# Queries and keys of two heads as block products through DRAM, with earlier copies out of PSUM and a later small load

## The chip, the cores and the metric

The kernel runs on one core of one Trainium2 chip. The metric is the device time in microseconds, the median of several runs; lower is better. Names in the rows: PE is the matrix engine (TensorE), PEld its weight load, DVE the vector engine, ACT the scalar engine, POOL and SP the two engines that issue the transfers (DMA).

## The reference

One step of a two-layer encoder on 576 tokens (64 of a running stream, 512 of a new one), width 2048, 16 heads of 128. Layer A is chunk-band attention with normed queries and keys, layer B attention over compressed keys and values; each layer adds its gated, projected result to its input.

```python
def a_project(h, w_in, g_q, g_k):
    q, k, v, g = jnp.split(h @ w_in, 4, axis=-1)
    hd = (b, s, A_HEADS, A_HEAD_DIM)
    return rmsnorm(q.reshape(hd), g_q), rmsnorm(k.reshape(hd), g_k), v.reshape(hd), g
...
    q, k, v, g = a_project(rmsnorm(x, ln), w_in, g_q, g_k)
    ...   # scores with a relative bias, softmax over the band, times v
    y = x + (jax.nn.silu(g) * o) @ w_out
    return y, k, v          # keys and values are outputs too
```

## The kernel before

Everything lies transposed, features in the 128 partitions and the 576 tokens along the free axis as two halves of 288. A float32 product is made of three products of rounded parts (high times high, low times high, high times low), so a **plain projection** of one 128-column tile is 16 k-tiles x 3 products x 2 halves = 96 matmuls of 128x288. Two such column tiles can be made together as a **block pair** (`block_pairs`): seven products of sums of blocks instead of eight, 7 x 8 x 3 = 168 matmuls instead of 192. Its inputs are sums of blocks of the activations, formed once beside earlier products (`block_operands`, tiles aiT, boT), and of the weights.

The stages of layer A: values and gates of heads 0 and 1 together (`values_and_gates`, banks av0, av1, ag0, ag1; ending at 60 us), the column sums of the layer norm (lnast) and their root chain, value and gate of head 2 as plain projections (ap34, ap50), then 13 block pairs (ai35 to ai47, to 393 us), each a value tile and a gate tile that are stored to DRAM (vd, sgd). After that `head_a` runs for each of 16 heads: queries and keys as plain projections (`proj`, a0p0, a0p1, ...), each with its norm (`qk_chain`: squares, sums over the partitions on PE as a00st, a01st, root, scaling, split into high and low parts qh, ql, kh, kl), the value loaded back from DRAM and transposed (`v_chain`), and the attention, whose pieces are laid between the projections of later heads. Then the output projection, layer B in the same style, and its output projection `out_b`: bo0 to bo3 plain, with the residual added (L1322), the other 12 tiles as block pairs bo4, bo6, ... .

PE's order is written out by hand: a small planner (`Order`) runs these routines as streams. A stream yields a bank class it needs ("mm": 2 banks of two halves, "st": 1, "x": 2), a time or a condition, and gets on when that is free by the planner's own clock; `od_.give` returns a bank after an assumed delay. The other engines' instructions are put in order by the scheduler of the language, and each engine and each queue works strictly in its order. Tiles come from pools with a fixed number of buffers for each tag, and a load into a tile waits until the buffer's last reader is done. In the head stage the tag raw (queries, keys and values) has 3 buffers.

Of the kernel before, what the change touches and what calls it, by code (L numbers as in the profile page):

```python
# [15 lines left out]
F32 = mybir.dt.float32  # L16
# [102 lines left out]
def encoder(tc, xT, wa_in, wa_out, wb_in, wuq, wuk, wuqr, wuv, wb_out, kcT, vc, ckvcT, krcT, gains, rtab,  # L119
# [26 lines left out]
    vd = dram.tile([D, N], F32, name="vd")  # L146
    sgd = dram.tile([D, N], F32, name="sgd")
    qrd = dram.tile([D, N], F32, name="qrd")
    qd = dram.tile([D, N], F32, name="qd")
# [493 lines left out]
    h, xs = [], []  # L643
    state = {"ln": 0.0, "scored": -1, "in": False}

# [40 lines left out]
    def out_of(m, src, y):  # L686
        (value_of if m < MG else gate_a)(m, src, y)

# [9 lines left out]
    def values_and_gates():  # L698
# [6 lines left out]
        for kt in range(KT):  # L705
            hi, lo = ws.get(3)
            for w in range(4):
                s = slice(w * P, (w + 1) * P)
                mm3(outs[w], (hi[:, s], lo[:, s]), [[x[:, c * 288:(c + 1) * 288] for x in h[kt]] for c in range(2)],
                    kt == 0, kt == KT - 1)  # L710
            yield None
            if kt + 4 < KT:
                load_x(kt + 4)
            square_sum(acc, xs[kt], tpx, N, kt == 0, f"lna{kt}")
        g1 = y_tile(MG + 1)
        ACT.copy(two(g1), pg1[:, :, :288])
# [5 lines left out]
        od_.spawn(1, stats_a(acc))  # L722
        for j in range(2):
            od_.spawn(1, later(MV + j, pv[j][:, :, :288], y_tile(MV + j), "mm"))
        od_.spawn(1, later(MG, two(g0), g0, None))
# [10 lines left out]
        for _ in form:  # L736
# [3 lines left out]
        pools.append(g_w1)  # L740
        yield from block_pairs(wa_in, X, [(MV + j, MG + j) for j in range(3, H)],
                               lambda name: wp1.tile([P, WH], F32, tag="o", bufs=10, name=name), None, y_tile,
# [22 lines left out]
    o2 = [None] * H  # L765
    ws = Weights(wload, [p for hd in range(H) for w in range(2) for p in parts_of(wa_in, [w * H + hd], "wa")], 2)

    def head_a(hd):
# [4 lines left out]
        def qk_chain(which, ps):  # L773
            col = gak if which else gaq
            raw = raw_of(ps, tpa, N, f"{n_}raw{which}")
            if which:
                kc = ap_.tile([P, NC], F32, tag="kc", bufs=2, name=n_ + "kc")
                nc.sync.dma_start(kc, kcT[hd * P:(hd + 1) * P, :])
            yield lambda: state["ln"]
            st = yield from halves(raw, tpa, N, f"{n_}{which}")  # L780
            t0 = max(od_.now, state["ln"] - 2.0)
            z = rnorm(st, P, N, base=EX, coef=P * EPS / D)
            scaled(raw, col, z)
            yield lambda: state["scored"] >= hd - 1
            if which == 0:
                hi = ap_.tile([P, N], F32R, tag="qh", bufs=1, name=n_ + "qh")
                lo = ap_.tile([P, N], F32R, tag="ql", bufs=1, name=n_ + "ql")
                split(raw, hi, lo)
            else:
                nc.gpsimd.dma_start(kT[hd * P:(hd + 1) * P, :], raw)  # L790
                hi = ap_.tile([P, NK], F32R, tag="kh", bufs=1, name=n_ + "kh")
                lo = ap_.tile([P, NK], F32R, tag="kl", bufs=1, name=n_ + "kl")
                split(raw, hi[:, NC:], lo[:, NC:])
                split(kc, hi[:, :NC], lo[:, :NC])
            yield max(t0 + L_RN, od_.now + L_SP)
            got[which] = hi, lo

        def v_chain():
            vt = tpa("raw", F32, n_ + "vt")
            nc.gpsimd.dma_start(vt, vd[hd * P:(hd + 1) * P, :])  # L800
# [14 lines left out]
            split(tps, vh, vl)  # L815
            od_.give("x", L_T)
            got["v"] = vh, vl, vs

# [4 lines left out]
        def bias():  # L823

            T = ap_.tile([P, 256], F32, tag="T", bufs=2, name=n_ + "T")
            nc.sync.dma_start(T, rtab[hd * P:(hd + 1) * P, :])
# [31 lines left out]
        for which in range(2):  # L858
            yield "mm"
            ps = ps_of("mm", f"{n_}p{which}")  # L860
            yield from proj(ps, ws, h, N)
            od_.spawn(1, qk_chain(which, ps))
# [171 lines left out]
    def rotary_key(ps):  # L1034
# [6 lines left out]
        split(raw, KR[0][:, NC:], KR[1][:, NC:])  # L1041
        cc = lp.tile([P, NC], F32, tag="cc", bufs=1, name="krc")
        nc.gpsimd.dma_start(cc, krcT)
# [257 lines left out]
    def pair_b(j):  # L1301

        t = []
        for kt in (j, j + 8):
            t.append(bo.tile([P, N], F32, tag="o", bufs=16, name=f"bf{kt}"))
            nc.gpsimd.dma_start(t[-1], od[kt * P:(kt + 1) * P, :])
        return t

    oB = Ahead((pair_b(j) for j in range(8)), 5)
    X, form_b, last_b = block_operands(lambda j: oB.get(), o2, bo, "bo")  # L1310

    def out_b():
        for m in range(4):
# [7 lines left out]
            y = out_tile_b(m)  # L1321
            V.tensor_tensor(out=two(y), in0=ps[:, :, :288], in1=two(xr), op=ALU.add)  # L1322
            od_.give("mm", L_M)
            done_b(m, y)
        last_b()
# [11 lines left out]
L_VT, L_G, L_CQ, L_M, L_V, L_LN, L_HA, L_LB = 5.0, 5.8, 10.0, 1.5, 5.0, 5.0, 8.0, 4.0  # L1337
ATT = "t0 s2 t1 s3 o-1 t2 t3"
DIRECT, GA, WRAW, WHL, SGB, DEEP, VA = 2, 2, 3, 5, 2, 2, 2
LAT = (0, 1, 2, 3, 8, 4, 5, 6, 7, 9, 10)  # L1340
# [86 lines left out]
```

## Time and profile before

| | us |
|---|---|
| median of 3 runs (2007.34 to 2012.24) | 2010.94 |
| the profiled execution | 2007.77 |
| its span, first to last instruction | 2005.9 |
| PE busy | 1956.2 (98%) |
| DVE busy | 1491.2 (74%) |
| ACT busy | 1180.6 (59%) |

The profile shows one execution. A row of a timeline has the start, the duration, the engine, the line, the operation with its output and inputs, and in brackets how long the engine sat idle before it and what ended that. Chains are read backwards: what ended last, and what released it. The granted clock is the share of full speed that PE had in a stretch.

### The profile page before, as it was taken

Reading aid. Unit: us, or ns where it says so; the run is one execution under the profiler, and the core shown is the slowest. Engines: PE = TensorE matmul, PEld = TensorE weight load, DVE = VectorE, ACT = ScalarE, POOL = GpSimd, SP = SyncE. Lnnn points to the kernel's source line nnn. Section 1 sums busy time; section 2 is a strip of 40 time slices with the busy share of each in tenths; the row PEclk is TensorE's granted clock in tenths of the full one; section 3 lists DMA queues with packets and bytes.
Section 4 is the critical chain, followed back from the end, with each engine's and each line's share of the span. In section 5 each row is a group of like instructions: output and inputs, shape, how many; then the busy total and the mean of one; then the engine's idle time right before and its main releaser. Section 6 shows DMA issues by size and latency. Waiting matters only on the chain.

```text
span 2005.9 us, 37809 instructions
## 1 busy us (share of the span) xinstructions
PE 1956.2 (98%) x14380; PEld 1932.3 (96%) x14380; DVE 1491.2 (74%) x2935; ACT 1180.6 (59%) x2214; POOL 136.9 (7%) x258
## 2 busy tenths in 40 slices
PE   8699999999999999999999899999999999999998
PEld 8699999999999999998999899999999999999998
DVE  8778888757777777779887648887776766776875
ACT  7655555556656565665544538986765666564332
POOL 1100000020000000000000200000000000002000
PEclk9899999999999999999999899999999999999999
DMA  7534444353222323222543525553222322256542
GB/s 232 190 117 135 141 133 134 120 198 92 91 91 88 98 81 99 84 92 66 190 148 108 182 80 147 161 165 117 78 84 88 91 86 83 83 153 222 168 143 64
DMA packets 125446, 247.00 MB, mean 123 GB/s; under 512 B 15808, under 2 KB 30160, under 8 KB 125264
## 3 DMA queue, kind: packets, MB, share of 16 engines
q1 hardware_dynamic: 104288, 171.46, 28.8%
q0 software_dynamic: 20976, 73.13, 10.5%
q8 instruction: 113, 1.85, 0.4%
q14 instruction: 69, 0.57, 0.1%
HBM read 198.07 MB, written 43.79 MB: 121 GB/s over the span
## 4 chain that ended last, share of the span: by engine, by line
PE 86%; issue 8%; DVE 2%; DMA 2%; ACT 1%; POOL 0%; SPq 0%; POOLq 0%; DVEq 0%; ACTq 0%
PE g L166 8%; PE lat L166 7%; PE u L166 4%; PE ao L166 2%; PE ap L166 1%; PE av L166 1%; PE a15p L166 1%; PE a14p L166 1%; PE a13p L166 1%; PE a12p L166 1%; PE a10p L166 1%; PE a9p L166 1%; PE a8p L166 1%; PE a7p L166 1%; PE a6p L166 1%
## 5 line engine op out<-in xcount | busy, mean ns | idle before, releaser
L206 DVE TENSOR_TENSOR wa_2l<-wa_2r,wa_2h 128x512 fp32r<-128x512 f32 x35 | 24.2, 691 | 19.7 <-ACT wa_2h L205 19.6
L205 ACT CAST wa_2h<-wa_2r 128x512 fp32r<-128x512 f32 x35 | 21.7, 620 | 21.4 <-PE a3p L166 1.9
L205 ACT CAST wa_0h<-wa_0r 128x512 fp32r<-128x512 f32 x35 | 21.5, 614 | 21.5 <-PE a0p L166 3.2
L206 DVE TENSOR_TENSOR wa_0l<-wa_0r,wa_0h 128x512 fp32r<-128x512 f32 x35 | 23.9, 684 | 11.7 <-ACT wa_0h L205 11.6
L206 DVE TENSOR_TENSOR wa_3l<-wa_3r,wa_3h 128x512 fp32r<-128x512 f32 x35 | 24.1, 687 | 11.1 <-ACT wa_3h L205 11.1
L206 DVE TENSOR_TENSOR wb_1l<-wb_1r,wb_1h 128x512 fp32r<-128x512 f32 x25 | 17.2, 688 | 15.0 <-ACT wb_1h L205 15.0
L166 PE MATMUL u<-cqh,wq_0h 128*128 128x288 f32 x128 | 27.7, 298 | 0.5 <-ACT q6raw L500 0.3
L205 ACT CAST wa_3h<-wa_3r 128x512 fp32r<-128x512 f32 x35 | 21.3, 609 | 10.4 <-PE a0p L166 4.4
L166 PE MATMUL u<-cqh,wq_0l 128*128 128x288 f32 x128 | 27.4, 296 | 0.0
L166 PE MATMUL u<-cql,wq_0h 128*128 128x288 f32 x128 | 27.3, 295 | 0.0
L206 DVE TENSOR_TENSOR wb_3l<-wb_3r,wb_3h 128x512 fp32r<-128x512 f32 x25 | 17.2, 687 | 13.2 <-ACT wb_3h L205 13.2
L166 PE MATMUL lat<-bh,wb_0h 128*128 128x288 f32 x88 | 19.9, 309 | 6.3 <-ACT bh L210 6.3
L205 ACT CAST wb_3h<-wb_3r 128x512 fp32r<-128x512 f32 x25 | 15.4, 616 | 17.8 <-PE lat L166 8.1
L205 ACT CAST wb_1h<-wb_1r 128x512 fp32r<-128x512 f32 x25 | 15.5, 618 | 17.5 <-PE lat L166 8.8
L206 DVE TENSOR_TENSOR wa_1l<-wa_1r,wa_1h 128x512 fp32r<-128x512 f32 x35 | 24.1, 689 | 2.0 <-ACT wa_1h L205 1.5
L166 PE MATMUL g<-bh,wb_1h 128*128 128x288 f32 x112 | 24.3, 298 | 0.0
L166 PE MATMUL g<-bh,wb_0h 128*128 128x288 f32 x112 | 24.3, 298 | 0.0
L166 PE MATMUL g<-bh,wb_2h 128*128 128x288 f32 x112 | 24.2, 298 | 0.0
L166 PE MATMUL g<-bh,wb_3h 128*128 128x288 f32 x112 | 24.2, 298 | 0.0
L166 PE MATMUL g<-bh,wb_0l 128*128 128x288 f32 x112 | 24.0, 296 | 0.0
L166 PE MATMUL g<-bh,wb_1l 128*128 128x288 f32 x112 | 24.0, 296 | 0.0
L166 PE MATMUL g<-bl,wb_1h 128*128 128x288 f32 x112 | 24.0, 296 | 0.0
(8217 smaller groups left out, 8616.4 us busy)
## 6 DMA issues: line engine op xcount, KB each, us to landing
wa_0r<-wa_in SPq DMA_DIRECT2D x34, 256.0 KB, 3.0
wa_1r<-wa_in SPq DMA_DIRECT2D x34, 256.0 KB, 3.1
wa_2r<-wa_in SPq DMA_DIRECT2D x34, 256.0 KB, 2.9
wa_3r<-wa_in SPq DMA_DIRECT2D x34, 256.0 KB, 3.0
wb_0r<-wb_in SPq DMA_DIRECT2D x25, 256.0 KB, 3.2
wb_1r<-wb_in SPq DMA_DIRECT2D x25, 256.0 KB, 3.2
wb_2r<-wb_in SPq DMA_DIRECT2D x25, 256.0 KB, 3.1
wb_3r<-wb_in SPq DMA_DIRECT2D x25, 256.0 KB, 2.9
```

Of the source, the lines that this page charges most:

```text
L166: nc.tensor.matmul(out, lhs, rhs, start=start, stop=stop, **kw)
L205: ACT.copy(hi, src)
L206: V.tensor_tensor(out=lo, in0=src, in1=hi.bitcast(F32), op=ALU.subtract)
```

## The change

- Heads 0 and 1 (`EARLY`) get their queries and keys from two more block pairs, (0, 16) and (1, 17), after the 13; `out_of` stores these raw to a new DRAM array qkd. Their four plain projections go, and `qk_chain` loads the raw tile from qkd (new tag rawd, 2 buffers) on POOL's queue.
- New conditions for the planner: at most 2 chains and 3 raws at a time, values in the order of the heads; the value tile has a buffer of its own (vt, 1), the bias table T 1 instead of 2.
- The first value's bank av0 is copied out by ACT with high priority, before the statistics; its scaling then reads the copy.
- The rotary key's cached part krc is loaded into a tile of the tag sw.
- In `out_b` the bank of bo0 to bo3 is copied out by ACT, and the residual is added afterwards from the copy; the tiles bf are all allocated at the start.

```diff
@@ -145,6 +145,7 @@
     od = dram.tile([D, N], F32, name="od")
     vd = dram.tile([D, N], F32, name="vd")
     sgd = dram.tile([D, N], F32, name="sgd")
+    qkd = dram.tile([2 * D, N], F32, name="qkd")
     qrd = dram.tile([D, N], F32, name="qrd")
     qd = dram.tile([D, N], F32, name="qd")
 
@@ -641,7 +642,7 @@
 
     ws = Weights(wload4, [(kt,) for kt in range(KT)], 2)
     h, xs = [], []
-    state = {"ln": 0.0, "scored": -1, "in": False}
+    state = {"ln": 0.0, "scored": -1, "in": False, "chains": 0, "raws": 0, "v": -1}
 
     def load_x(kt):
         x = tpx("x", F32, f"x{kt}")
@@ -684,7 +685,10 @@
         nc.gpsimd.dma_start(sgd[hd * P:(hd + 1) * P, :], y)
 
     def out_of(m, src, y):
-        (value_of if m < MG else gate_a)(m, src, y)
+        if m < MV:
+            nc.gpsimd.dma_start(qkd[m * P:(m + 1) * P, :], y)
+        else:
+            (value_of if m < MG else gate_a)(m, src, y)
 
     def y_tile(m):
         return tpy("y", F32, f"y{m}")
@@ -712,6 +716,10 @@
             if kt + 4 < KT:
                 load_x(kt + 4)
             square_sum(acc, xs[kt], tpx, N, kt == 0, f"lna{kt}")
+        v0 = y_tile(MV)
+        with tc.high_priority():
+            ACT.copy(two(v0), pv[0][:, :, :288])
+        od_.give("mm", L_M)
         g1 = y_tile(MG + 1)
         ACT.copy(two(g1), pg1[:, :, :288])
         od_.give("st", L_M)
@@ -720,8 +728,8 @@
             ACT.copy(g0[:, c * 288:(c + 1) * 288], pg0[c][:, :288])
             od_.give("x", L_M)
         od_.spawn(1, stats_a(acc))
-        for j in range(2):
-            od_.spawn(1, later(MV + j, pv[j][:, :, :288], y_tile(MV + j), "mm"))
+        od_.spawn(1, later(MV, two(v0), v0, None))
+        od_.spawn(1, later(MV + 1, pv[1][:, :, :288], y_tile(MV + 1), "mm"))
         od_.spawn(1, later(MG, two(g0), g0, None))
         od_.spawn(1, later(MG + 1, two(g1), g1, None))
         oX = Ahead((pair_x(j) for j in range(8)), 1)
@@ -738,7 +746,7 @@
         close(g_x)
         g_w1, wp1 = pool("wblocks")
         pools.append(g_w1)
-        yield from block_pairs(wa_in, X, [(MV + j, MG + j) for j in range(3, H)],
+        yield from block_pairs(wa_in, X, [(MV + j, MG + j) for j in range(3, H)] + [(hd, H + hd) for hd in EARLY],
                                lambda name: wp1.tile([P, WH], F32, tag="o", bufs=10, name=name), None, y_tile,
                                lambda m, y: out_of(m, two(y), y), "ai")
 
@@ -763,7 +771,8 @@
         V.memset(t[:, :256], 0.0)
         nbA.append(t)
     o2 = [None] * H
-    ws = Weights(wload, [p for hd in range(H) for w in range(2) for p in parts_of(wa_in, [w * H + hd], "wa")], 2)
+    ws = Weights(wload, [p for hd in range(H) if hd not in EARLY for w in range(2)
+                          for p in parts_of(wa_in, [w * H + hd], "wa")], 2)
 
     def head_a(hd):
 
@@ -772,15 +781,26 @@
 
         def qk_chain(which, ps):
             col = gak if which else gaq
-            raw = raw_of(ps, tpa, N, f"{n_}raw{which}")
+            if ps is None:
+                yield lambda: state["scored"] >= hd - 2
+                raw = ap_.tile([P, N], F32, tag="rawd", bufs=2, name=f"{n_}raw{which}")
+                r0 = (which * H + hd) * P
+                nc.gpsimd.dma_start(raw, qkd[r0:r0 + P, :])
+            else:
+                yield lambda: state["raws"] < 3
+                state["raws"] += 1
+                raw = raw_of(ps, tpa, N, f"{n_}raw{which}")
             if which:
                 kc = ap_.tile([P, NC], F32, tag="kc", bufs=2, name=n_ + "kc")
                 nc.sync.dma_start(kc, kcT[hd * P:(hd + 1) * P, :])
             yield lambda: state["ln"]
+            yield lambda: state["chains"] < 2
+            state["chains"] += 1
             st = yield from halves(raw, tpa, N, f"{n_}{which}")
             t0 = max(od_.now, state["ln"] - 2.0)
             z = rnorm(st, P, N, base=EX, coef=P * EPS / D)
             scaled(raw, col, z)
+            state["chains"] -= 1
             yield lambda: state["scored"] >= hd - 1
             if which == 0:
                 hi = ap_.tile([P, N], F32R, tag="qh", bufs=1, name=n_ + "qh")
@@ -792,11 +812,14 @@
                 lo = ap_.tile([P, NK], F32R, tag="kl", bufs=1, name=n_ + "kl")
                 split(raw, hi[:, NC:], lo[:, NC:])
                 split(kc, hi[:, :NC], lo[:, :NC])
+            if ps is not None:
+                state["raws"] -= 1
             yield max(t0 + L_RN, od_.now + L_SP)
             got[which] = hi, lo
 
         def v_chain():
-            vt = tpa("raw", F32, n_ + "vt")
+            yield lambda: state["v"] >= hd - 1 and state["scored"] >= hd - 2
+            vt = ap_.tile([P, N], F32, tag="vt", bufs=1, name=n_ + "vt")
             nc.gpsimd.dma_start(vt, vd[hd * P:(hd + 1) * P, :])
             vs = ap_.tile([P, 2, P], F32, tag="vs", bufs=2, name=n_ + "vs")
             nc.sync.dma_start(vs[:, 0, :], vc[hd * P:(hd + 1) * P, :])
@@ -814,6 +837,7 @@
             vl = ap_.tile([P, 512], F32R, tag="vl", bufs=1, name=n_ + "vl")
             split(tps, vh, vl)
             od_.give("x", L_T)
+            state["v"] = hd
             got["v"] = vh, vl, vs
 
         sg = op_.tile([P, N], F32, tag="o", bufs=16, name=n_ + "sg")
@@ -822,7 +846,7 @@
 
         def bias():
 
-            T = ap_.tile([P, 256], F32, tag="T", bufs=2, name=n_ + "T")
+            T = ap_.tile([P, 256], F32, tag="T", bufs=1, name=n_ + "T")
             nc.sync.dma_start(T, rtab[hd * P:(hd + 1) * P, :])
             nb = nbA[hd % 2]
             nbs = ap_.tile([P, PK], F32, tag="nbs", bufs=1, name=n_ + "nbs")
@@ -856,9 +880,11 @@
 
         od_.spawn(0, attend())
         for which in range(2):
-            yield "mm"
-            ps = ps_of("mm", f"{n_}p{which}")
-            yield from proj(ps, ws, h, N)
+            ps = None
+            if hd not in EARLY:
+                yield "mm"
+                ps = ps_of("mm", f"{n_}p{which}")
+                yield from proj(ps, ws, h, N)
             od_.spawn(1, qk_chain(which, ps))
         od_.spawn(1, v_chain())
 
@@ -1039,7 +1065,7 @@
         rope(raw, "kr")
         nc.gpsimd.dma_start(krT, raw[:64, :])
         split(raw, KR[0][:, NC:], KR[1][:, NC:])
-        cc = lp.tile([P, NC], F32, tag="cc", bufs=1, name="krc")
+        cc = tpl("sw", F32, "krc")[:, :NC]
         nc.gpsimd.dma_start(cc, krcT)
         split(cc, KR[0][:, :NC], KR[1][:, :NC])
 
@@ -1302,9 +1328,11 @@
 
         t = []
         for kt in (j, j + 8):
-            t.append(bo.tile([P, N], F32, tag="o", bufs=16, name=f"bf{kt}"))
+            t.append(bf[kt])
             nc.gpsimd.dma_start(t[-1], od[kt * P:(kt + 1) * P, :])
         return t
+
+    bf = [bo.tile([P, N], F32, tag="o", bufs=16, name=f"bf{kt}") for kt in range(KT)]
 
     oB = Ahead((pair_b(j) for j in range(8)), 5)
     X, form_b, last_b = block_operands(lambda j: oB.get(), o2, bo, "bo")
@@ -1319,8 +1347,10 @@
                 ps = ps_of("mm", f"bo{m}")
                 yield from beside(proj(ps, wo, o2, N), form_b, 4)
             y = out_tile_b(m)
-            V.tensor_tensor(out=two(y), in0=ps[:, :, :288], in1=two(xr), op=ALU.add)
+            with tc.high_priority():
+                ACT.copy(two(y), ps[:, :, :288])
             od_.give("mm", L_M)
+            V.tensor_tensor(out=y, in0=y, in1=xr, op=ALU.add)
             done_b(m, y)
         last_b()
         yield from block_pairs(wb_out, X, [(m, m + 1) for m in range(4, KT, 2)], raw_b, residual_b, out_tile_b,
@@ -1336,6 +1366,7 @@
 
 L_VT, L_G, L_CQ, L_M, L_V, L_LN, L_HA, L_LB = 5.0, 5.8, 10.0, 1.5, 5.0, 5.0, 8.0, 4.0
 ATT = "t0 s2 t1 s3 o-1 t2 t3"
+EARLY = 0, 1
 DIRECT, GA, WRAW, WHL, SGB, DEEP, VA = 2, 2, 3, 5, 2, 2, 2
 LAT = (0, 1, 2, 3, 8, 4, 5, 6, 7, 9, 10)
 LAHEAD = 1
```

PE at the end of the values, before: the last gate matmuls (ag1), the column sums (lnast, two halves of two matmuls each), then ap34.

```order
L166 MATMUL ag1_171<-hl15_640,wa_15h_647 128x288 x2
L166 MATMUL ag1_171<-hh15_639,wa_15l_648 128x288 x2
L166 MATMUL lnast_772<-lnas2_768,ones_79 128x288 x2
L166 MATMUL lnast_772<-lnas3_769,ones_79 128x288 x2
L166 MATMUL ap34_808<-hh0_126,wa34_0h_810 128x288 x2
L166 MATMUL ap34_808<-hl0_127,wa34_0h_810 128x288 x2
```

And now, the place where ap34 starts and the place of the sums:

```order
L167 MATMUL ag1_172<-hh15_640,wa_15l_649 128x288 x2
L167 MATMUL ap34_774<-hh0_127,wa34_0h_776 128x288 x2
L167 MATMUL ap34_774<-hl0_128,wa34_0h_776 128x288 x2
...
L167 MATMUL ap34_774<-hl4_203,wa34_1h_782 128x288 x2
L167 MATMUL ap34_774<-hh4_202,wa34_1l_783 128x288 x2
L167 MATMUL lnast_861<-lnas2_770,ones_80 128x288 x2
L167 MATMUL lnast_861<-lnas3_771,ones_80 128x288 x2
L167 MATMUL ap34_774<-hh5_240,wa34_1h_782 128x288 x2
```

Thirty matmuls of ap34 (five k-tiles) have moved ahead of the column sums.

POOL's queue at the start of the head stage, before: the last of 16 gate loads (a0sg to a15sg, which follow one another directly), head 0's value, the first key store.

```order
L820 DMA a14sg_10480<-sgd_72 128x576
L820 DMA a15sg_10895<-sgd_72 128x576
L800 DMA a0vt_5149<-vd_71 128x576
L790 DMA kT<-a0raw1_5137 128x576
L800 DMA a1vt_5500<-vd_71 128x576
L790 DMA kT<-a1raw1_5488 128x576
```

And now, from the stores of the two new block pairs on (y0 and y1 are queries, y16 and y17 keys):

```order
L689 DMA qkd_73<-y0_4862 128x576
L689 DMA qkd_73<-y16_4863 128x576
L689 DMA qkd_73<-y1_5126 128x576
L788 DMA a0raw0_5391<-qkd_73 128x576
L689 DMA qkd_73<-y17_5127 128x576
L788 DMA a0raw1_5401<-qkd_73 128x576
L823 DMA a0vt_5413<-vd_71 128x576
L844 DMA a0sg_5385<-sgd_72 128x576
```

Between that and the next piece stand more gate loads, a1vt and a2vt.

```order
L844 DMA a12sg_9696<-sgd_72 128x576
L844 DMA a13sg_10111<-sgd_72 128x576
L788 DMA a1raw0_5417<-qkd_73 128x576
L844 DMA a14sg_10526<-sgd_72 128x576
L844 DMA a15sg_10941<-sgd_72 128x576
L810 DMA kT<-a0raw1_5401 128x576
L788 DMA a1raw1_5419<-qkd_73 128x576
```

Head 0's raws are loaded between the stores and the gate loads; head 1's come behind most of the gate loads, and its key behind the store of head 0's key (kT).

ACT around the key of head 0 and the squares of head 1, before (a01sq: root steps of head 0's key; a10sq: squares of head 1's query):

```order
L485 ACTIVATE a01sq_5141<-a01st_5250 128x576
L486 ACTIVATE a01s2_5143<-a01sq_5141 128x576
L488 ACTIVATE a01sq_5141<-a01s2_5143 128x576
L205 CAST wa2_0h_5375<-wa2_0r_5374 128x512
L500 COPY a1raw0_5303<-a1p0_5153 128x576
L450 ACTIVATE a10sq_5305<-a1raw0_5303 64x576
L451 ACTIVATE a10s3_5306<-a1raw0_5303 64x576
L205 CAST a0kh_5261<-a0raw1_5137 128x576
L453 CAST a10s2_5307<-a10sq_5305 64x576
```

And now, from the root steps of head 0's key on:

```order
L486 ACTIVATE a01sq_5405<-a01st_5606 128x576
L487 ACTIVATE a01s2_5407<-a01sq_5405 128x576
L489 ACTIVATE a01sq_5405<-a01s2_5407 128x576
L206 CAST wa3_1h_5753<-wa3_1r_5752 128x512
L206 CAST a0kh_5617<-a0raw1_5401 128x576
L451 ACTIVATE a10sq_5550<-a1raw0_5417 64x576
L452 ACTIVATE a10s3_5551<-a1raw0_5417 64x576
L454 CAST a10s2_5552<-a10sq_5550 64x576
L451 ACTIVATE a11sq_5623<-a1raw1_5419 64x576
L452 ACTIVATE a11s3_5624<-a1raw1_5419 64x576
L486 ACTIVATE a10sq_5550<-a10st_5682 128x576
```

The copies of head 1's raws out of PSUM (L500) are gone; the squares of head 1's query now stand behind the cast of head 0's key, and those of its key ahead of the root steps of its query.

## Rows read from the trace of the kernel before

**Rows 1.** The page, part 4: the chain that ended last, by engine.

```profile
PE 86%; issue 8%; DVE 2%; DMA 2%; ACT 1%; POOL 0%; SPq 0%; POOLq 0%; DVEq 0%; ACTq 0%
```

**Rows 2.** PE's waits: what it waited for, us in total, times, longest.

```profile
PE lnast L166 <- ACT y L716: 7.9, 1, 7.9
PE ap L166 <- DVE y L676: 7.3, 1, 7.3
PE lat L166 <- ACT bh L210: 6.3, 2, 3.7
...
PE bo L166 <- DVE by L1322: 3.4, 1, 3.4
PE bo4a L166 <- DVE bo4p10l L206: 2.9, 1, 2.9
PE a0vts L170 <- DMA a0vt<-vd: 1.8, 1, 1.8
```

**Rows 3.** The chain in order of time: start, us, engine, work, count.

```profile
76.81 27.42 PE ap L166 x192
...
393.28 21.60 PE a0p L166 x162
...
1118.20 6.58 DMA krc<-krcT
```

**Rows 4.** Windows: length, busy PE, PEld, DVE, ACT, POOL, clock, DMA share, GB/s.

```profile
77.00:81.00 4.00, 4.00 (x20) 4.00 (x20) 3.93 (x8) 2.82 (x6) 2.14 (x4) 0.59 0.93 311
85.00:104.00 19.00, 19.00 (x145) 19.00 (x144) 10.04 (x15) 4.46 (x8) 1.61 (x3) 1.00 0.49 163
459.00:919.00 460.00, 460.00 (x3419) 454.10 (x3420) 339.37 (x786) 285.84 (x586) 15.13 (x28) 1.00 0.29 90
1834.00:1837.00 3.00, 2.85 (x14) 2.85 (x15) 3.00 (x8) 0.43 (x1) 2.05 (x4) 0.63 0.63 194
```

**Rows 5.** The timeline from 60 to 77 us, at the end of the values.

```profile
62.95 0.77 ACT L661 ACTIVATE xx<-xx,gn 128x576 f32<-128x576 f32 x1 [1.79 <-DMA xx<-xT]
...
64.63 0.60 ACT L205 CAST wa_3h<-wa_3r 128x512 fp32r<-128x512 f32 x1
...
67.48 0.63 ACT L716 COPY y<-ag 128x576 f32<-128x576 f32 x1
...
68.16 1.33 PE L166 MATMUL lnast<-lnas,ones 128*128 128x288 f32 x4 [7.86 <-ACT y L716]
...
76.00 1.42 DVE L676 TENSOR_TENSOR y<-av,rs 128x576 f32<-128x576 f32 x2
```

**Rows 6.** The timeline from 406 to 424 us: the chain of head 0's query.

```profile
407.04 0.69 ACT L450 ACTIVATE a00sq<-a0raw 64x576 f32<-64x576 f32 x1
...
409.94 0.76 DVE L454 TENSOR_TENSOR a00s<-a00sq,a00s 64x576 fp32r<-64x576 f32 x1 [0.74 <-ACT a00s L453]
...
414.72 0.43 PE L166 MATMUL a00st<-a00s,ones 128*128 128x288 f32 x2
...
418.34 0.76 DVE L489 SCALAR_TENSOR_TENSOR a00sq<-a00st,a00sq 128x576 f32<-128x576 f32 x1 [1.29 <-ACT a00sq L488]
...
420.41 0.81 DVE L496 SCALAR_TENSOR_TENSOR a0raw<-a0raw,gs,a00sq 128x576 f32<-128x576 f32 x1
...
422.22 0.76 DVE L206 TENSOR_TENSOR a0ql<-a0raw,a0qh 128x576 fp32r<-128x576 f32 x1
```

**Rows 7.** Transfers issued from 390 to 440 us: KB, median us to landing.

```profile
a0sg<-sgd POOLq DMA_DIRECT2D x1, 288.0 KB, 3.4
...
a8sg<-sgd POOLq DMA_DIRECT2D x1, 288.0 KB, 9.3
...
kT<-a0raw POOLq DMA_DIRECT2D x1, 288.0 KB, 2.5
```

**Rows 8.** The timeline from 1830 to 1865 us, DVE in the output projection.

```profile
1833.34 0.76 DVE L1322 TENSOR_TENSOR by<-bo,bxr 128x576 f32<-128x576 f32 x1 [6.18 <-DMA bxr<-x1d]
...
1863.38 0.69 DVE L206 TENSOR_TENSOR bo4p10l<-bo4r,bo4p10h 128x512 fp32r<-128x512 f32 x1
```

## The prediction

> **What bounds the kernel now.** I read the page's shares first, then TensorE's waits, then the chain, and only then single stretches. TensorE (PE) is 86% of the chain that ended last, and no other engine or transfer over 2% [rows 1]. So a saving counts only if PE does less, waits less, or runs slowly for a shorter time. The waits of PE add up to a few dozen microseconds, and the reader should see in [rows 2] that they are few and single: 7.9 and 7.3 us at the end of the values stage, 6.3 at the start of layer B (two waits), 3.4 and 2.9 in the output projection, 1.8 at head 0's value transposes. In the middle of the attention there is none: from 459 to 919 us PE is busy for all of 460 us, while DVE is busy 339.37 us [rows 4], 74%. That stretch cannot absorb a delay: a stall put ahead of it moves everything behind it.
>
> The profiled execution took 2007.77 us, 3.2 below the median of the runs shown (2010.94). Terms are worked out inside the profiled one, and their sum is put on the median. About 0.3% (6 us) is what a measurement of this kernel can tell from no change.
>
> **Part 1: fewer products.** The four projections of heads 0 and 1 were 4 x 96 = 384 matmuls; two more block pairs are 2 x 168 = 336. 162 projection matmuls took 21.60 us [rows 3], 0.1333 each, so 48 fewer are **-6.4 us**. PE does them in an unbroken row before and after, so nothing hides this.
>
> **Part 2: the first value bank is freed early.** In the old order PE ends the values at 60.3, waits 7.86 us for a gate's copy (L716, 67.48) [rows 5], does the 4 column-sum matmuls, waits again until both the statistics and the first value's scaling (L676, at 76.00) are through, and starts ap34 at 76.81 [rows 3]. In the new order, 30 matmuls of ap34 stand ahead of the sums and need only value 0's bank. Its copy stands on ACT right behind the cast of wa34's fourth part, which ran 64.63 to 65.23 [rows 5]; with the 0.63 us of L716's copy it ends at about 65.8, and ap34 starts at 65.9. Then: 192 matmuls at 0.1325 (the 145 of 85 to 104 us took 19.00, [rows 4]) are 25.4; the sums 0.7. After the old idle the granted clock over 77 to 81 was 0.59 (mostly at the lower of its two levels, 1.2 GHz) and PE did 20 matmuls in 4 us instead of 30 [rows 4], 1.3 lost, 1.5 with the first ones before 77; the wait of 3.4 us [rows 2] was enough elsewhere (0.63 over 1834 to 1837, [rows 4]), so behind the new idle of 5.6 us I charge 1.5 again. ap50 needs value 1's bank, freed by the scaling that waits for the statistics: these took 76.00 - 68.16 = 7.8 us from the sums [rows 5]; the sums now come at about 71.5 and some casts of ap50's weights stand between, so scaling is through near 81 against PE's arrival near 80.5; I charge 1.0 (0 to 2). The end is 65.9 + 25.4 + 0.7 + 1.5 + 1.0 = 94.5 against 76.81 + 27.42 = 104.2 [rows 3]: **-9.7 us** (-7.6 to -10.6). The cover this needs: the blocks' operands, formed beside ap34 and ap50, must be ready 10 us sooner; DVE was busy 10.04 and ACT 4.46 of the 19 us before 104 [rows 4], so there are 9 us to give.
>
> **Part 3: the output projection.** ACT now copies the bank, and the bank no longer waits for the residual's load, which held DVE's L1322 (6.18 us idle, at 1833.34) and PE until 1834.15 [rows 2, 8]. So bo2 starts about 3.4 sooner and at the full clock (14 matmuls took 2.85 us there instead of 1.9, [rows 4]: 1.0 lost). That would be 4.4. But PE waits again at bo4a, 2.91 us, for DVE's bo4p10l at 1863.38 [rows 2, 8], and DVE worked without a break from 1833.34. What DVE does there is the forming of block operands, gated by the loads of od that follow the last gate's store, not by PE. So PE comes sooner to the same late neighbour. The gain is 0 if DVE's row starts where it did and 3.5 if it starts as soon as the load can land; I take **-2**.
>
> **Part 4: the later krc load.** Of PE's two waits there (6.3, the longest 3.7, so the other 2.6 [rows 2]) the shorter hangs on a cast of krc, a load of 64 KB that landed after 6.58 us [rows 3]. In the new order the load of the first cached latents, as large, stands in exactly its place on POOL's queue, and its cast in the same place on ACT, between the same two casts PE waits for. I take **0**. At worst the rotary key's second half, now near its use, adds 2.
>
> **Part 5: heads 0 and 1 through DRAM, the loss.** Let Y be the time at which PE does head 0's query sums (a00st). The old trace gives all steps of a chain after it: L484 to L489 frees the sums' only bank at +4.4, L496 (scaling) starts at +5.7, and the low part ql ends at +8.3 (414.72 to 422.98) [rows 6]. The new raws have two buffers and stand in one queue, POOL. Head 1's query (a1raw0) takes the buffer of head 0's query, free when ql is made: issue at Y+8.3. Landing is bounded by 3.4 us (a0sg, the first of a burst) and 9.3 (a8sg, in its middle) [rows 7]; I take the near end, because the four gate loads just ahead were issued some 3 us before. Landed at Y+11.8. ACT works in order, and has head 0's key cast (a0kh) ahead: PE reaches a01st at Y+5.3 (30 matmuls and head 1's transposes), its scaling ends 6.5 later, and the cast is done at Y+12.8. Squares to sums take 3.7 (407.04 to 410.70, [rows 6]): ready at Y+16.5. PE arrives, after 36 more matmuls of a2p1, at Y+10.5: a stall of **6.0**, and 1.5 for the slow clock behind it. Head 1's key (a1raw1) follows a store of head 0's key, which lands 2.5 us after its issue [rows 7], at Y+14.3; the load lands at Y+17.9. ACT has its squares ahead of head 1's query root steps, so the bank of a10st comes free only at about Y+24.2, and PE arrives at Y+23.2: 1.0. Behind that, four chains and two heads' scores meet in DVE: the four chains alone are 28 steps of about 0.76 [rows 6], 21 us, in a stretch where PE had 25 us of two projections; I charge 2 (0 to 5). The wait for head 0's values goes from 1.8 [rows 2] to about 0.7 (issued 2.1 us after the last block, an estimated landing of 4.2, PE there after 42 matmuls, 5.6). Sum **+9.4**, from +3 (loads early, DVE's work alone) to +16 (landing at 7 or more, twice).
>
> The Trainium skill, "DMA: Bandwidth & Descriptors", "Anatomy of one DMA", fits a POOL-issued transfer as about 2.0 us plus its bytes at 436 GB/s; for these 288 KB that is an estimate of 2.7 us. The rows of this case have 2.5 for a lone store but 3.4 to 9.3 in the burst, so the trace agrees only where the queue is quiet. By the page the second load would land 0.7 us sooner and the sum would be under 1 us lower; the first stall stays, since ACT's order sets it.
>
> **Sum:** -6.4 - 9.7 - 2 + 9.4 = -8.7. The profiled execution would be 1999.1, the median 2002.2; I say **2002.3 us**.
>
> **Rivals.**
> A. *The loads hide.* If raws land early and ACT's order happens to leave room, the attention's start costs only DVE's own work, +3: -6.4 - 9.7 - 2 + 3 = -15.1, 1996. For: PE had no stall there but 1.8. Against: the two buffers tie head 1's load to head 0's ql, whatever the queue does.
> B. *Slower.* The same tie with the burst's landing time. At 9.3 us each, a1raw0 lands at Y+17.6 and the first stall is 10.8; a1raw1 is 5.9 later than taken, 6.9 in all; the clock stays low for all 36 matmuls between (3.9), with 1.5 once more, and DVE adds 5. With the 0.7 for 1.8 that is +27: total about +9, 2020. It decides from a start that costs over 24 us. Against: the burst's first transfers are done by then.
> C. *The values' gain is lost.* If the blocks' operands (or their raw weights) are not formed earlier, PE waits in front of ai35 until about 104, and the sum is -6.4 - 2 + 9.4 = +1: 2012. Against: the idle half of DVE there [rows 4]. For: the loads of x for the forming came in a slow rhythm, ACT's L661 waited for one just before 62.95.
>
> **How the numbers follow.** Forecast 0.54 (0.36 of it faster by over 0.3%, 0.18 within), A 0.20 (faster), C 0.14 (within), B 0.12 (0.10 slower, 0.02 within). Faster 0.56, same 0.34, slower 0.10. The bounds of the terms add up to -16.5 (1994) and +4 (2015); leaving out B and the worst ends, I give 1994 to 2012.
>
> **What would show it.** The products: 14268 matmuls instead of 14316. Part 2: ap34 starts near 66, not 76.8, and ai35 near 94.5; an idle ahead of ai35 is C. Part 3: PE's wait at bo2 gone, that at bo4a grown to 4 to 6 us. Part 4: PE's second wait at the start of layer B still some 2.6 us. Part 5: new PE waits at a10st of about 6 us and at a11st of about 1, with granted clock near 0.5 behind the first; if both are under 1, it is A; if they are 10 and 7, it is B. A wait at heads 2 or 3 would be one that I have not seen.

## The result and the profile after

| | before | changed |
|---|---|---|
| median, us | 2011.22 (4 runs, 2007.34 to 2012.24) | 2023.1 (4 runs, 2022.4 to 2024.54) |
| profiled execution, us | 2007.77 | 2024.54 |
| its span, us | 2005.9 | 2022.5 |

The ratio of changed to before is 1.0066, interval [1.0051, 1.0081]: slower, by 12 us or 0.6%. The forecast was 2002.3, faster, with a range that ended at 2012.

PE did fewer matmuls and was busy about as long as before (1956.2 us then). Part 1 of the page, by engine busy us, share of the span and instructions:

```profile
PE 1955.1 (97%) x14332; PEld 1927.6 (95%) x14332; DVE 1511.1 (75%) x2969; ACT 1190.3 (59%) x2235; POOL 141.2 (7%) x266
```

48 matmuls are gone, which should have been 6.4 us of busy time, yet only 1.1 went: some of the remaining ones ran more slowly. The rest of the time is in waits. PE's waits (us in total, times, longest), to be held against [rows 2]:

```profile
PE ap L167 <- ACT y L721: 7.5, 1, 7.5
PE bo4a L167 <- DVE bo4p10l L207: 7.3, 1, 7.3
PE a10st L167 <- DVE a10s L455: 7.3, 1, 7.3
PE lat L167 <- ACT bh L211: 6.5, 2, 3.5
...
PE a0vts L171 <- DMA a0vt<-vd: 2.8, 1, 2.8
PE v0v L167 <- ACT b0kraw L501: 2.1, 1, 2.1
PE r1st L167 <- DVE q1sq L490: 1.8, 1, 1.8
PE a0s L167 <- DVE ptl L207: 1.7, 2, 1.0
...
PE ai35a L167 <- ACT y L412: 1.3, 1, 1.3
...
PE ai35a L167 <- DVE y L414: 1.2, 1, 1.2
PE a11st L167 <- DVE a10sq L490: 1.1, 1, 1.1
```

Of the waits in [rows 2], that at the column sums and that at bo2 are gone, as the prediction had it. In their place stand a10st, a11st, v0v, r1st, two in ai35a, many under 1 us at the first heads' scores, and 4.4 us more at bo4a.

Where in the program the time went is read best from the same marks in both timelines, the start of PE's first matmul of each (us of the profiled executions):

| mark | before | changed | difference |
|---|---|---|---|
| ap34 | 76.81 | 66.38 | -10.4 |
| ai35, the first block pair | 104.06 | 95.02 | -9.0 |
| end of the 13 old block pairs | 393.12 | 387.08 | -6.0 |
| first latent of layer B | 1120.02 | 1127.93 | +7.9 |
| r1st (layer B, queries) | 1226.92 | 1236.66 | +9.7 |
| b1k (layer B, keys of head 1) | 1374.72 | 1389.54 | +14.8 |
| bo4c (output projection) | 1868.46 | 1884.62 | +16.2 |

So the values stage gained what was forecast; 3 us were given back in the first block pair; the heads of layer A, with their two new block pairs, lost 14 instead of 3; layer B lost 7; between layer B's heads and bo4c 1 us more went. (The profiled execution of the changed kernel is the slowest of the four, 1.4 above their median; that of the kernel before is 3.5 under its own. So about 5 of the 16.6 us between the two profiles are the choice of execution, and the differences by stage are that uncertain.)

### The profile page after: what moved, and what is told of

Read it like the earlier page. It is cut to its first block, busy times and chain, and to the rows that moved or that the text cites. A ratio compares the mean times of both kernels' runs of the same rounds, so it can differ in the third digit from the quotient of the medians.

```text
span 2022.5 us, 37807 instructions
## 1 busy us (share of the span) xinstructions
PE 1955.1 (97%) x14332; PEld 1927.6 (95%) x14332; DVE 1511.1 (75%) x2969; ACT 1190.3 (59%) x2235; POOL 141.2 (7%) x266
## 5 line engine op out<-in xcount | busy, mean ns | idle before, releaser
L207 DVE TENSOR_TENSOR wb_3l<-wb_3r,wb_3h 128x512 fp32r<-128x512 f32 x25 | 17.2, 687 | 16.8 <-ACT wb_3h L206 16.6
L207 DVE TENSOR_TENSOR wb_2l<-wb_2r,wb_2h 128x512 fp32r<-128x512 f32 x25 | 17.1, 686 | 11.0 <-ACT wb_2h L206 11.0
L167 PE MATMUL g<-bh,wb_1h 128*128 128x288 f32 x112 | 24.3, 298 | 0.0
L167 PE MATMUL g<-bh,wb_0h 128*128 128x288 f32 x112 | 24.3, 298 | 0.0
L167 PE MATMUL g<-bh,wb_3l 128*128 128x288 f32 x112 | 24.0, 296 | 0.0
```

Of the source, the lines that this page charges most:

```text
L167: nc.tensor.matmul(out, lhs, rhs, start=start, stop=stop, **kw)
L207: V.tensor_tensor(out=lo, in0=src, in1=hi.bitcast(F32), op=ALU.subtract)
```

## The experiments

The runs have short names: free_raws, no_early, no_krc, av_only (the early copy alone), plain_all (no early head, krc in its place), spread (heads 5 and 10), one, outb_only, cover_spread and cover_start (projections done as well), guards_only (the conditions alone) and av_guards, in the order of the sections. All are timed against the kernel before on the same chip; its medians in the three groups of runs were 2010.8 (free_raws to av_only), 2010.2 (plain_all to outb_only) and 2011.5 (the rest), so a difference between runs of two groups is uncertain by about 1 us more. Head-stage figures below are the way from the end of the 13 old block pairs to layer B's first latent, profiled, against before (changed kernel: +7.9 + 6.0 = +14.0).

### Head 1's loads set free

```diff
-                raw = ap_.tile([P, N], F32, tag="rawd", bufs=2, name=f"{n_}raw{which}")
+                if hd:
+                    yield lambda: state["raws"] < 3
+                    state["raws"] += 1
+                raw = ap_.tile([P, N], F32, tag="raw" if hd else "rawd", bufs=3 if hd else 2, name=f"{n_}raw{which}")
...
-            if ps is not None:
+            if ps is not None or hd:
                 state["raws"] -= 1
```

> The changed kernel with one difference: head 1's raw query and key take two of the three buffers of the tag raw, idle at that time, so their loads no longer wait for head 0's chain. Theory 'tie' (the stall at a10st comes from the two shared buffers): PE's wait of 7.3 us at a10st and the 2.3 us of low clock behind it go, 9 to 11 us less than the changed kernel, about 2013. Rival 'dense' (DVE and ACT have too much to do for four chains and two heads' scores in that stretch, whatever the loads do): the waits move to the later sums and scores, under 4 us less, 2019 to 2022.

Measured: 2016.8 (ratio to before 1.0027 [1.0017, 1.0036]), 6.3 less than the changed kernel; head stage +7.1 instead of +14.0. The tie is real: in the changed kernel head 1's query is loaded only when head 0's low part (a0ql) is made, and PE stands for it. The timeline of the changed kernel (start, duration, engine, line, operation, idle before):

```profile
453.55 0.75 DVE L207 TENSOR_TENSOR a0ql<-a0raw,a0qh 128x576 fp32r<-128x576 f32 x1
...
454.60 0.54 POOL L788 DMA_DIRECT2D a1raw<-qkd  x1 [2.62 <-DVE a0ql L207]
...
457.26 0.82 DVE L497 SCALAR_TENSOR_TENSOR a0raw<-a0raw,gs,a01sq 128x576 f32<-128x576 f32 x1
458.11 0.67 ACT L206 CAST a0kh<-a0raw 128x576 fp32r<-128x576 f32 x1 [2.44 <-DVE a0raw L497]
...
459.63 0.68 ACT L451 ACTIVATE a10sq<-a1raw 64x576 f32<-64x576 f32 x1 [0.85 <-DMA a1raw<-qkd]
...
462.52 0.75 DVE L455 TENSOR_TENSOR a10s<-a10sq,a10s 64x576 fp32r<-64x576 f32 x1 [0.74 <-ACT a10s L454]
...
463.42 0.82 PE L167 MATMUL a10st<-a10s,ones 128*128 128x288 f32 x2 [7.26 <-DVE a10s L455]
```

With free buffers the wait at a10st is gone. But half of the 14.0 us stays in the head stage, and of what the early heads cost in all (26, next section) three quarters. PE's waits in this run:

```profile
PE a0vts L171 <- DMA a0vt<-vd: 4.0, 1, 4.0
...
PE a0s L167 <- DVE ptl L207: 1.6, 2, 0.9
PE a1s-1_6071 L167 <- DVE ptl L207: 1.5, 1, 1.5
PE a11st L167 <- DVE a10sq L490: 1.5, 1, 1.5
```

and the stretch in which all four chains run (window; length, then busy PE, PEld, DVE, ACT, POOL, clock, DMA share, GB/s):

```profile
452.00:465.00 13.00, 12.20 (x92) 11.90 (x90) 12.32 (x19) 11.06 (x19) 5.30 (x10) 1.00 0.87 292
```

DVE is busy 12.32 of 13 us there: the rival had its share too. Neither theory alone was right.

### No early head

```diff
-EARLY = 0, 1
+EARLY = ()
```

> The changed kernel with no head taken early (the list EARLY empty): queries and keys of heads 0 and 1 are plain projections again, all other edits stay, the planner's new conditions too. Theory: the head stage loses about 21 us by the loads and chains and gains 6.4 by fewer products, so without it the time falls by 14: about 2009. Rival: the new conditions and the single buffers of vt and T cost part of the 21 themselves; then it stays above 2013.

Measured: 2003.5 (0.996 [0.9946, 0.9974]). The early heads cost 19.6 us net, 26 with the 6.4 that their products save. It is below both expectations, since the head stage came out at -3.0, under the kernel before: the new conditions gain.

### krc back in its place

```diff
-        cc = tpl("sw", F32, "krc")[:, :NC]
+        cc = lp.tile([P, NC], F32, tag="cc", bufs=1, name="krc")
```

> The changed kernel with krc back in its own tile (loaded before the latents). PE's order is the same. Theory 'krc': the 6 us lost between the start of layer B and head 1's keys (waits of 1.8 at r1st and 2.1 at v0v with the slow clock behind it) come from ACT's and DVE's order around the later krc; back to about 2017. Rival: they come from something else in that stretch (ACT's order for other reasons): 2022 to 2024.

Measured: 2019.7 (1.0041 [1.0028, 1.0054]), 3.4 less, between the theory and its rival; without early heads the same edit is worth 3.5 (no_early 2003.5 against plain_all 2000.0, below; 2.9 when each is held against the before of its own group). These sizes are near the runs' scatter (the six runs of no_krc lie between 2013 and 2022). The wait at r1st goes in both. In the changed kernel the load stands right ahead of its cast; ACT waits 1.33 us for it, and has behind it the squares of r1 and the root steps of q1 (q1sq), which PE waits for at r1st:

```profile
1226.83 0.56 POOL L1069 DMA_DIRECT2D krc<-krcT  x1
...
1230.32 0.30 ACT L206 CAST KRh<-krc 128x128 fp32r<-128x128 f32 x1 [1.33 <-DMA krc<-krcT]
...
1230.53 0.68 ACT L466 ACTIVATE r1sq<-r1raw 128x576 f32<-128x576 f32 x1
...
1232.79 0.73 ACT L479 ACTIVATE q1sq<-q1st,epst 128x576 f32<-128x576 f32 x1
...
1236.66 0.50 PE L167 MATMUL r1st<-r1s,blk 128*128 128x288 f32 x2 [1.75 <-DVE q1sq L490]
```

With krc in its place the same step of q1 came 1.8 us sooner, though ACT's work ahead of it lay within 0.2 us of the above:

```profile
1230.95 0.74 ACT L479 ACTIVATE q1sq<-q1st,epst 128x576 f32<-128x576 f32 x1
```

The wait of 2.1 us at v0v shrank to 0.7; in free_raws and no_early, which have the late krc too, it is not among the larger waits, and in cover_spread (below), which has not, it is 1.9. So I do not put it down to krc.

### Only the early copy of av0

```diff
+        v0 = y_tile(MV)
+        with tc.high_priority():
+            ACT.copy(two(v0), pv[0][:, :, :288])
+        od_.give("mm", L_M)
...
-        for j in range(2):
-            od_.spawn(1, later(MV + j, pv[j][:, :, :288], y_tile(MV + j), "mm"))
+        od_.spawn(1, later(MV, two(v0), v0, None))
+        od_.spawn(1, later(MV + 1, pv[1][:, :, :288], y_tile(MV + 1), "mm"))
```

> The kernel before with the early copy of av0 alone. Theory: ai35 starts 9 us earlier, the first blocks give 3 of these back, the rest stays: 6 us less than before, 2005. Rival A: the 3 us in the first blocks come from the other edits, and 9 stay: 2002. Rival B: the gain is lost later in the head stage: 2010 to 2012.

Measured: 2005.5 (0.9969 [0.9956, 0.9982]), 5.4 less than before. ai35 starts at 95.92, the 13 pairs end at 388.00: 8.1 gained, 3.0 given back. The operands of the first block pair were ready; what came late is the bank. In both kernels ACT has the first steps of ap50's gate ahead of the copy that frees the bank of ai35a, and they wait for DVE's first step of that gate. Before, DVE stood ready and did it when PE was through with ap50:

```profile
104.26 0.76 DVE L506 TENSOR_TENSOR y<-ap,rs 128x576 f32<-128x576 f32 x1 [1.34 <-PE ap L166]
...
107.69 0.38 ACT L411 COPY y<-ai35a 128x288 f32<-128x288 f32 x1
```

In the changed kernel DVE has stood 3.95 us ahead of value 2 (y<-ap, L677) and then works off what is behind it, head 1's gate (ag49) and sums of weight blocks. It comes to ap50's gate 4 us after the last matmuls of ap50 (94.75), and PE waits:

```profile
89.75 0.76 DVE L677 TENSOR_TENSOR y<-ap,rs 128x576 f32<-128x576 f32 x1 [3.95 <-DMA vd<-y]
...
95.72 0.75 DVE L514 TENSOR_TENSOR y<-y,ag49u 128x576 f32<-128x576 f32 x1
...
99.02 0.75 DVE L507 TENSOR_TENSOR y<-ap,rs 128x576 f32<-128x576 f32 x1
...
101.68 0.77 ACT L511 ACTIVATE ag50u<-ag50u,onet 128x576 f32<-128x576 f32 x1
...
102.36 0.37 ACT L412 COPY y<-ai35a 128x288 f32<-128x288 f32 x1
...
102.79 0.40 PE L167 MATMUL ai35a<-aiT6h,ai35p60h 128*128 128x288 f32 x1 [1.28 <-ACT y L412]
```

The second wait in ai35a (1.2, at 116.96) is for an addition on DVE (L414) that follows sums of the next pair's weight blocks; ap50's gate has long left DVE (104.37). In the run with the early copy alone the two waits are 0.4 and 1.9.

### No early head, krc in its place

Both edits above (EARLY empty, tile cc).

> The changed kernel without early heads and with krc in its old tile: what is left are the early copy of av0, the planner's conditions and the output projection's copies. Theory: krc's 2 us at r1st come off the run without early heads (2003.5), and nothing else: 2001 to 2002, 9 us under the kernel before. Rival: krc costs nothing by itself, 2003 to 2004.

Measured: 2000.0 (0.9947 [0.9931, 0.9963]): 10 us faster than the kernel before and 23 than the changed kernel. The only edit between it and no_early is krc's.

### Two early heads elsewhere

```diff
-EARLY = 0, 1
+EARLY = 5, 10
```

with krc in its place.

> As plain_all, but with heads 5 and 10 early instead of 0 and 1: the same two block pairs and DRAM round trips, at two places inside the head stage. Theory 'density' (what remains of the loss with the buffers freed, some 13 us, is the start: the burst of loads, and two heads in a row without projections to lay their chains and scores beside): far from the start the loss falls to a few us, so with 6.4 fewer us of products the time is near or under plain_all, 1997 to 2004. Rival 'any head': a head without its projections starves PE by as much wherever it stands (DVE does 23.6 us of work per head, PE's attention alone has 7): some 6 to 10 us over plain_all, 2008 to 2012.

Measured: 2017.9 (1.0036 [1.0023, 1.005]), 17.9 over plain_all: the density theory falls, and the loss is well over what the rival priced (6 to 10 over plain_all). Two heads in the middle of the stage, far from the burst and with no tie, lose 24 with their products counted. The waits, the same at both heads (a5, a10 their own sums; a4, a9 the scores of the head before):

```profile
PE a101st L167 <- DVE a100sq L490: 3.0, 1, 3.0
PE a51st L167 <- DVE a50sq L490: 2.8, 1, 2.8
PE a4s L167 <- DVE ptl L207: 2.2, 2, 1.5
PE a9s L167 <- DVE ptl L207: 2.2, 2, 1.5
...
PE a9s L167 <- DVE a9pts L561: 1.0, 1, 1.0
PE a4s L167 <- DVE a4pts L561: 1.0, 1, 1.0
```

No load is among them, nor behind them: head 5's raws are loaded some 150 us before they are first read.

```profile
L788 POOL DMA_DIRECT2D a5raw<-qkd x2: 541/542/543, 436.0 to 436.5; - x2
L451 ACT ACTIVATE a50sq<-a5raw x1: 682/682/682, 590.5 to 590.5; 64x576 f32<-64x576 f32 x1
```

DVE and ACT are late, and neither is full, as this window shows (first spread, then plain_all, where both do as much or more and PE never stands):

```profile
600.00:660.00 60.00, 52.10 (x357) 50.02 (x356) 42.39 (x95) 33.23 (x69) 3.78 (x7) 0.94 0.30 92
600.00:660.00 60.00, 60.00 (x446) 59.21 (x445) 43.29 (x95) 37.84 (x76) 2.16 (x4) 1.00 0.33 92
```

### One early head

```diff
-EARLY = 0, 1
+EARLY = (0,)
```

with krc in its place.

> As plain_all, but head 0 alone is early. The two buffers then hold its query and key and no load waits for a chain. If the loss were all the tie of head 1 to head 0, one head would show the bare gain of 3.2 us: 1998 to 1999. If the start itself costs (values late, no projections of head 0 to cover its chains), one head costs about half of the two: 2004 to 2008.

Measured: 2003.7 (0.996 [0.9946, 0.9974]), 3.8 over plain_all, so a loss of 7 with 3.2 saved. No tie exists here. One head at the very start costs less than one in the middle (12 each). A reason that fits, though no run tests it, is that there is no earlier head whose scores lie bare: PE's new waits are at head 0's own sums (a00st 2.8, a01st 2.6), none at scores. The second head at the start, without the tie, then adds 12 to 13 (free_raws is 13.3 over no_early, 19.7 with the products), as much as one in the middle.

### Only the copies in the output projection

```diff
+            with tc.high_priority():
+                ACT.copy(two(y), ps[:, :, :288])
-            V.tensor_tensor(out=two(y), in0=ps[:, :, :288], in1=two(xr), op=ALU.add)
             od_.give("mm", L_M)
+            V.tensor_tensor(out=y, in0=y, in1=xr, op=ALU.add)
```

and the tiles bf allocated at the start.

> The kernel before with only the copies in the output projection. Theory: PE's wait at bo2 (3.4 us) goes and that at bo4a grows by as much, since DVE's row of block operands sets when bo4a can start: within 1 us of before, 2010 to 2012. Rival: DVE starts its row as much sooner, 3 to 5 us less, 2006 to 2008.

Measured: 2010.8 (1.0003 [0.9994, 1.0012]), level. What bounds the stage is DVE's row of block operands, and that waits for the loads of od. In the changed kernel, the idle time of DVE ahead of its sums of bf, by what ended it:

```profile
L296 DVE TENSOR_TENSOR bf<-bf,bf 128x288 f32<-128x288 f32 x16 | 7.2, 452 | 4.7 <-DMA bf<-od 4.7
L296 DVE TENSOR_TENSOR bf<-bf 128x288 f32<-128x288 f32 x16 | 7.2, 453 | 2.3 <-DMA bf<-od 2.3
```

### The early heads' projections done as well

```diff
-    ws = Weights(wload, [p for hd in range(H) if hd not in EARLY for w in range(2)
+    ws = Weights(wload, [p for hd in range(H) for w in range(2)
...
-            if hd not in EARLY:
-                yield "mm"
-                ps = ps_of("mm", f"{n_}p{which}")
-                yield from proj(ps, ws, h, N)
+            yield "mm"
+            ps = ps_of("mm", f"{n_}p{which}")
+            yield from proj(ps, ws, h, N)
+            if hd in EARLY:
+                od_.give("mm", L_M)
+                ps = None
```

> As spread (heads 5 and 10 early), but their four plain projections are done as well and thrown away: 384 matmuls, 51.2 us, back in the row of PE, with the stores, loads and chains through DRAM unchanged. Theory 'cover' (an early head costs because PE has no projection of its own to lay between the attention pieces and the norm chains): PE's waits in the head stage go, and the time is plain_all plus two block pairs of 22.2 us: 2000 + 44.5 = 2044 to 2047. Rival 'round trip' (the stores, loads and queue order cost): the waits stay, 2018 + 51 = 2069.

Measured: 2049.2. 51.2 us of matmuls were added and the time rose by 31.3: of the loss of 24.3 (2017.9 - 2000.0 + 6.4), 19.5 to 20 vanish, although every store, load and chain through DRAM is still there; 4.8 stay over the 2044.4 of plain_all plus two block pairs. That is 2 us above the theory's range and 20 under the rival. In the same window as above, which holds head 5's chains in both runs, PE does 449 matmuls without a gap where it did 357 with gaps, and DVE and ACT do as much work:

```profile
600.00:660.00 60.00, 60.00 (x449) 59.35 (x449) 41.84 (x102) 32.73 (x70) 3.23 (x6) 1.00 0.38 100
```

> The changed kernel with krc in its old tile and the four projections of heads 0 and 1 done as well and thrown away. Theory 'cover': the stall at a10st (7 us), that at a0vts and the small ones behind them are hidden by the projections, 2044 to 2048. Rival 'round trip': the waits for the loads stay, 2020 + 51 = 2071.

Measured: 2051.0, 31.3 over no_krc for the same 51.2. At heads 0 and 1 too, the projections hide the round trip, the tie included (a10st is not among the waits), but for one wait of 4.6 at head 0's first transpose; the time is 3 above the theory's range.

Putting the projections back also gives DVE and ACT 51 us more for the same work, so by itself the test does not tell missing cover from engines short of time. For heads 5 and 10 the windows above tell it: DVE does the same work in 60 us in plain_all while PE never stands. At the start DVE was near full for a while (12.32 of 13 us in free_raws), so there both may have a share.

### Only the planner's conditions

The kernel before with the conditions on chains, raws and values and the buffers of vt and T.

> The kernel before with only the planner's new conditions and the buffers vt and T, no head early. Theory: plain_all (10 us faster) is the sum of the early copy of av0 (5) and of these conditions, which take away the wait for head 0's value and 2 to 3 us more: 2005 to 2007. Rival: the conditions do nothing alone, 2010.

Measured: 2007.1 (0.9978 [0.9969, 0.9988]), 4.4 less than before; head stage -3.0. With a buffer of its own the first value no longer waits for a raw: its load is issued at 395.15, ahead of the gate loads, where it was issued at 419.01, behind them, in the kernel before, and the 1.8 us wait of [rows 2] is gone. Which of the conditions and buffers bring the rest, this run does not tell.

```profile
395.15 0.54 POOL L819 DMA_DIRECT2D a0vt<-vd  x1
```

### The early copy and the conditions, without the output projection's copies

> plain_all without the copies in the output projection. Theory: those copies are worth nothing (outb_only was level with before), so this is level with plain_all, 1999 to 2002. Rival: they are worth 2 to 4 us once the rest is faster, 2002 to 2004.

Measured: 1999.3 (0.994 [0.9923, 0.9957]), level with plain_all's 2000.0. The copies are worth nothing here either.

## Why the prediction was wrong

The sum by single edits, in medians: products -6.4; av0 -5.4; conditions -4.4; output projection 0; krc +3.5; what the early heads lose, +26.0 (no_early against the changed kernel, 19.6, plus 6.4). That makes +13.3 against +12 measured. By the steps of the prediction:

1. **Products, -6.4.** Right in kind and size: 14332 instructions on PE instead of 14380, and the 336 matmuls of the two new block pairs took 44.42 us (387.08 to 431.50), 0.132 each.
2. **Values, -9.7.** Right up to ai35: ap34 at 66.38 (forecast 65.9), ai35 at 95.02 (94.5). Then wrong by 3: the operands were formed in time, but that DVE had "9 us to give" did not hold. Its idle time of before lay ahead of the first block pair; now DVE came to the pair with work left over, and ap50's gate, which stands in the pair in both kernels, came later in it. In the first 9 us of the pair (before, then changed) DVE (the third busy figure) went from 7.19 to 8.71 busy and PE from 9.00 to 7.72:

```profile
104.00:113.00 9.00, 9.00 (x70) 9.00 (x69) 7.19 (x11) 6.83 (x12) 0.54 (x1) 1.00 0.33 97
95.00:104.00 9.00, 7.72 (x59) 7.49 (x58) 8.71 (x15) 5.54 (x11) 0.54 (x1) 1.00 0.33 94
```

   Net -6.0 in the profile, -5.4 alone.
3. **Output projection, -2.** The mechanism was right (PE comes sooner to the same late neighbour), the value was the wrong end: 0. The 3.4 us at bo2 went, and 4.4 came at bo4a.
4. **krc, 0.** The part on the old place was right: as large a load took it, and the wait there stayed (6.3 before, 6.5 now). I gave the new place 0 to 2 and took 0; the medians put it at 2.9 to 3.5, of which the profile shows 1.8, as PE's wait at r1st behind ACT's cast.
5. **Heads 0 and 1, +9.4 ahead of the products.** This is the step that failed: the term measured +26.0. The tie was close: the stall at a10st was 7.3 (6.0 forecast), that at a11st 1.1 (1.0), with the clock at 0.50, its lower level, behind the first. These were priced 8.5 together, and freeing the buffers is worth 6.3 (free_raws). Two details in it were off: ACT's order did not set the first stall, as forecast, but the load, for which ACT waited another 0.85 us behind its cast; and the wait for head 0's value was 2.8, not 0.7. What was wrong by far is the line "I charge 2 (0 to 5)" for what comes behind: the 19.7 that are left of the 26.0. I counted DVE's work against PE's and found them near each other; but PE's waits do not need a full DVE. A head's chains and scores are steps that wait for one another across PE, ACT and DVE, and the old order hides a head's chains and the scores of the head before under that head's own projections, 25.6 us of work that waits for nothing here. Taking the projections away uncovers the steps. Two windows of the changed kernel, the slow clock behind a10st and the bare scores behind it:

```profile
463.50:468.00 4.50, 4.50 (x19) 4.50 (x20) 1.27 (x2) 1.90 (x3) 0.04 (x1) 0.50 0.24 66
476.00:490.00 14.00, 11.85 (x84) 11.07 (x84) 12.65 (x32) 8.81 (x22) 0.55 (x1) 1.00 0.30 84
490.00:510.00 20.00, 17.67 (x126) 16.77 (x127) 14.30 (x34) 11.69 (x25) 0.54 (x1) 1.00 0.27 76
```

   In the last two, PE idles 4.5 of 34 us at the full clock. spread shows this loss without the start, the burst or the tie (24), and cover_spread takes 20 of it away by putting the projections back. The tie is a second, separate cause: 6 to 7 us (free_raws). That most of the loss comes of taking the projections away, and not of the round trip, is shown; how it divides at the start between bare steps and a DVE that is full for a while is not.
6. **Conditions, no term.** They were in the list of the change and had no price. They gained 4.4, of which 3 are seen in the head stage; where the rest lies was not settled, and run-to-run differences of the values stage (ap34 between 65.8 and 69.2 in kernels with the same code there) are as large.

Of the rivals, B (slower) had the right sign and the wrong mechanism: the loads of head 1 landed in 4.0 us (median of two), not 9; that its price of +27 is so near the 26 found is luck. The bound of +16 for the head start excluded what happened, because it was built from loads alone. (The lower bound of the whole was added up wrongly: -6.4 - 10.6 - 3.5 + 3 is -17.5, not -16.5; nothing hangs on it.) The sentence that the middle of the attention "cannot absorb a delay" was read correctly, and its other half was missed: PE is busy for 460 of 460 us there because each head brings its own cover.

What stays open: whether another order on PE, with pieces of an early head laid beside later heads' projections, would hide the bare steps, which no run tries; how the 24 us of spread divide between recorded waits (some 15 us more idle than plain_all in that stage) and matmuls that ran longer (some 6 us); the 5 to 7 us that remain with the projections put back; and about 5 of the 7 us that layer B lost in the profile of the changed kernel. From r1st to b1k it took 152.9 us, before 147.8, but free_raws and no_early, with the same late krc, 147.9 and 149.2.

## What to carry to other kernels

Matmuls that wait for nothing are also the cover for everything that waits: before taking them away, ask which chain of small steps they hide, and price the chain bare, step by step, not by the busy shares of its engines. A cheap test of such a saving is to keep the work and throw its result away: if the loss goes, the new path is not what costs; whether cover was missing or another engine had too little time must then be read from the busy shares. And price every edit of a change, the bookkeeping ones too: here the planner's conditions and their buffers gained 4.4 us, the copies at the end of the kernel nothing.

## What the runs showed that I had not expected

Two early heads lose about as much in the middle of the stage (24) as at the start (26), though the start has the burst of loads, the tie and, for a while, DVE nearly full; without the tie the start loses 19.7. The early transfer of a bank out of PSUM gained 5.4 where PE's next work was ready and 0 where it was not, with the same copy of 0.63 us.
